# A hybrid decoder layer on one core: the low parts of the down weights by an accumulating DMA instead of a VectorE subtraction

## The chip, the cores and the metric

The kernel runs on one core of a Trainium2 chip. The core has TensorE (matmuls, into PSUM), VectorE, ScalarE and GpSimd (elementwise work), SyncE (SP, which here only issues DMAs), and 16 DMA engines that move data between HBM and the on-chip SBUF. Each engine works through its own queue of instructions in order and waits on semaphores for what other engines and DMAs produce. In the profile the engines are called PE (PEld for its weight loads), DVE, ACT, POOL and SP. The metric is the time on the device, in microseconds (us), as the median of runs; a profile is one execution of the same program, recorded instruction by instruction.

## The reference

One layer of a decoder over 256 tokens of width 1024, in float32:

```python
xn = rms_norm(x, attn_norm_g)
proj = xn @ w_in                        # one projection for both head groups
x = x + concat([y_moba, y_gla]) @ w_out # block attention and gated linear attention
hn = rms_norm(x, ffn_norm_g)
h = causal_dwconv(hn @ w_ffn_up, conv_w, conv_b)     # 2 * 2816 columns, 3 taps
x = x + (silu(h[..., :2816]) * h[..., 2816:]) @ w_ffn_down   # 2816 -> 1024
return rms_norm(x, final_norm_g)
```

The change lies in the last product, with `w_ffn_down` (2816 x 1024).

## The kernel before

**Matmuls in three parts.** TensorE takes operands of type float32r, which keep fewer bits than float32. To come close to float32, each operand is split into a high part (a copy rounded to float32r) and a low part (the operand minus its high part, again as float32r). A product is then three matmuls (`mm3`, lines 113 to 116): high by high (L114), high by low (L115) and low by high (L116), summed in PSUM. In a row such as `L115 PE MATMUL acc<-dlo,gh`, `gh` is the stationary operand and `dlo` the moving one.

**Stages.** The input projection, the two attentions and the output projection take the first 110 us or so; the FFN then runs to about 300 us. There the 2816 columns are cut into NP = 22 tiles of 128. For tile i:

- `ups[i]`, the 1 MB of up weights (128 x 2048), comes by DMA from SP into one of four `raw` buffers; ScalarE writes `hi` (L97) and VectorE `lo` (L100), in halves. The end of an up tile's second `lo` lets SP load the next up tile (`load_next`).
- `up_mm(i, ...)` multiplies them with the normed activations (`hh`, `hl`) into a PSUM bank `att`, 48 matmuls.
- VectorE rescales the result (`conv_u`, L845, or L848 in halves), ScalarE and VectorE do the convolution (`conv_a` L855, `conv_b` L863, silu L866), `gate_hi` multiplies the halves (L870) and writes the rounded gate `gh` on ScalarE (L873), `gate_lo` the rest `gl` on VectorE (L878).
- `dload(i)` has SP load the 512 KB of down weights (128 x 1024) into one of three `draw` buffers (L794). `dhi(i)` lets ScalarE write the high part into one of four `dhi` buffers (L800), `dlo(i)` lets VectorE subtract and write the low part into one of four `dlo` buffers (L805).
- `down_mm(i, tt, n)` multiplies gate and down weights for token half tt and bank n; five calls of three matmuls per tile, summed over all tiles in PSUM banks `dacc` that already hold the residual.

**Order.** In the FFN every queue's order is written out by hand; nothing is reordered. Tile 0 to 3 are unrolled (lines 938 to 1006), the rest is the loop at line 1008. In pass i TensorE does `up_mm(i)` and then `down_mm(i - 3)`; pass 4 does the down product of tiles 0 and 1 both. The other engines, in the same pass, finish tile i - 1: its conv and gate, `dhi(i - 1)` between the convolution and the gate, `dlo(i - 1)` at the end. Near the end, pass 20 also holds `dload(21)`, `dhi(20)` and `dlo(20)`, pass 21 has `dhi(21)`, and `dlo(21)` follows `conv_b(21, 1)`. After the last pass come the down products of the last four tiles, then the final norm and the stores.

**Buffers.** `dload(i)` overwrites the buffer of raw tile i - 3, so SP holds it, and everything behind it in SP's queue, until the reads of that tile by `dhi(i - 3)` and `dlo(i - 3)` are done. GpSimd has no work in the FFN.

The first tiles' order, as written (lines 980 to 1006, calls on the changed path and around it):

```python
    dhi(0); ids(1); gate_hi(0); dlo(0); gate_lo(0)               # pass 2
    ...
    hi(5, 0); conv_bb(1); conv_u(2, None); ids(2); lo(5, 0); hi(5, 1); gate_hi(1); dhi(1)   # pass 3
    conv_bb(2); gate_lo(1); gate_hi(2); dhi(2); lo(5, 1); gate_lo(2); dlo(1); dlo(2)
```

Of the kernel before, what the change touches and what calls it, by code (L numbers as in the profile page):

```python
# [12 lines left out]
AF = mybir.ActivationFunctionType  # L13
ALU = mybir.AluOpType
# [20 lines left out]
def trunk_kernel(ctx: ExitStack, tc: tile.TileContext, xT_d, wG_d, w5_d, wo_d, up_d, dn_d,  # L35
                 par_d, gla_g_d, fin_g_d, wgu_d, cos_d, sin_d, causal_d, lvl_d, ident_d, out_d):
    nc = tc.nc
    V, A, T, DMA = nc.vector, nc.scalar, nc.tensor, nc.sync
# [751 lines left out]
    downs = {}  # L790
# [6 lines left out]
    def dhi(i):  # L797
        hi = ff.tile([128, D], F32R, name="dhi", bufs=4)
        lo = ff.tile([128, D], F32R, name="dlo", bufs=4)
        A.activation(hi, downs[i][0], AF.Copy)  # L800
        downs[i] += [hi, lo]

    def dlo(i):
        d, hi, lo = downs[i]
        V.tensor_sub(lo, d, hi)  # L805

    finb = ff.tile([128, D], F32, name="finb")
    rb = ff.tile([128, S], F32, name="rb")
# [169 lines left out]
    lo(4, 1)  # L978
    conv_bb(0)
    dhi(0)  # L980
    ids(1)
    gate_hi(0)
    dlo(0)
    gate_lo(0)

# [10 lines left out]
    hi(5, 1)  # L996
    gate_hi(1)
    dhi(1)
    conv_bb(2)
    gate_lo(1)  # L1000
    gate_hi(2)
    dhi(2)
    lo(5, 1)
    gate_lo(2)
    dlo(1)
    dlo(2)

    for i in range(4, NP):
# [57 lines left out]
    for tt in range(2):  # L1066
# [4 lines left out]
        for n in range(BANKS[tt]):  # L1071
            d = dacc[tt, n]
# [91 lines left out]
```

## Time and profile before

| | before |
|---|---|
| median of 2 runs | 308.04 us (308.02 to 308.06) |
| profiled execution: span | 306.0 us |
| outside the span, against the median | 2.04 us |
| PE busy in the span | 298.6 us (98%) |
| DVE, ACT, POOL busy | 244.6, 207.3, 4.4 us |
| moved by DMA | 55.33 MB |
| low parts of the down weights (L805, DVE) | 22 x 1219 ns = 26.7 us |
| high parts of the down weights (L800, ACT) | 22 x 1047 ns = 23.0 us |

The span runs from the first to the last instruction of the profiled execution, and no time for that execution other than its span is recorded. Busy time of the engines overlaps, so the columns don't add up. In a row of a group of instructions stand line, engine, operation, output and inputs by the program's names, count, then busy time, mean duration in ns, and the idle time of the engine just before, with what ended it. In a timeline row stand start and duration in us, then engine, line, operation and names; a bracket at its end gives the idle time before it and what ended it.

### The profile page before, as it was taken

The page shows a single profiled execution, that of the slowest core. Times are in us where ns is not written, and L with a number is a line of the kernel's source. Part 1 is how long each engine was busy: PE and PEld are TensorE (multiplying, and loading weights), DVE is VectorE, ACT ScalarE, POOL GpSimd, SP SyncE. Part 2 cuts the span into 40 slices and gives each one's busy share as a digit, 9 for nine tenths or more (in the row PEclk, how much of TensorE's full clock was granted, in tenths as well). Part 3 has the DMA queues.
Part 4 walks back from the last instruction along what each step waited for, and adds up shares of the span by engine and source line. Part 5 has one row for each costly group of instructions (what it writes and reads, how often), then busy time and mean ns, then how long its engine had stood idle before and what let it go on. Part 6 is the DMA issues. An engine that isn't in the chain of part 4 may idle for free.

```text
span 306.0 us, 6251 instructions
## 1 busy us (share of the span) xinstructions
PE 298.6 (98%) x2498; PEld 282.4 (92%) x2498; DVE 244.6 (80%) x456; ACT 207.3 (68%) x385; POOL 4.4 (1%) x21
## 2 busy tenths in 40 slices
PE   8999999999999999999999999999999999999992
PEld 8999998777889999999999999999999999999992
DVE  4697998999487699799999977778888777776652
ACT  4897999898998477657677755555566665534362
POOL 2000100000000000000000000000000000000000
PEclk9999999999999999999999999999999999999999
DMA  6997855263553452981566665444444722110003
GB/s 185 372 338 283 298 177 184 97 256 141 173 203 135 179 188 72 418 349 57 200 256 256 263 216 202 161 174 167 161 178 198 274 71 69 71 69 2 0 0 138
DMA packets 12300, 55.33 MB, mean 181 GB/s; under 512 B 1376, under 2 KB 3184, under 8 KB 8048
## 3 DMA queue, kind: packets, MB, share of 16 engines
q1 hardware_dynamic: 12128, 54.81, 48.9%
q8 instruction: 19, 0.31, 0.4%
q10 hardware_dynamic: 144, 0.13, 0.1%
q14 instruction: 9, 0.07, 0.1%
HBM read 53.89 MB, written 1.05 MB: 180 GB/s over the span
## 4 chain that ended last, share of the span: by engine, by line
PE 89%; DMA 3%; ACT 3%; DVE 2%; SPq 1%; issue 1%; ACTq 0%; DVEq 0%
PE att L114 14%; PE att L116 14%; PE att L115 14%; PE acc L114 14%; PE acc L116 13%; PE acc L115 13%; DMA raw<-in_wG 3%; PE att L388 1%; DVE lo L100 1%; PE att L524 1%; ACT hi L97 1%; PE att L570 1%; PE att L452 1%; PE att L590 1%; ACT ah L181 1%
## 5 line engine op out<-in xcount | busy, mean ns | idle before, releaser
L97 ACT ACTIVATE hi<-raw 128x1024 fp32r<-128x1024 f32 (+3 forms) x88 | 79.9, 933 | 43.4 <-PE att L115 37.5
L100 DVE TENSOR_TENSOR lo<-raw,hi 128x1024 fp32r<-128x1024 f32 (+4 forms) x90 | 93.5, 1056 | 14.9 <-ACT hi L97 14.8
L114 PE MATMUL att<-hh,hi 128*128 128x256 f32 x352 | 98.5, 280 | 0.0
L115 PE MATMUL att<-hl,hi 128*128 128x256 f32 x352 | 98.2, 279 | 0.0
L116 PE MATMUL att<-hh,lo 128*128 128x256 f32 x352 | 98.2, 279 | 0.0
L114 PEld LDWEIGHTS att<-hh,hi 128*128 128x128 f32 x352 | 66.2, 188 | 0.1
L115 PEld LDWEIGHTS att<-hl,hi 128*128 128x128 f32 x352 | 66.2, 188 | 0.0
L116 PEld LDWEIGHTS att<-hh,lo 128*128 128x128 f32 x352 | 66.2, 188 | 0.0
L863 DVE SCALAR_TENSOR_TENSOR c<-us,par,c 128x256 f32<-128x256 f32 x88 | 40.7, 482 | 4.1 <-ACT c L855 2.5
L855 ACT ACTIVATE c<-us,par 128x256 f32<-128x256 f32 x44 | 24.0, 591 | 22.3 <-DVE us L845 17.0
L115 PE MATMUL acc<-dlo,gh 128*128 128x512 f32 (+1 forms) x88 | 32.2, 365 | 0.0
L116 PE MATMUL acc<-dhi,gl 128*128 128x512 f32 (+1 forms) x88 | 32.1, 365 | 0.0
L114 PE MATMUL acc<-dhi,gh 128*128 128x512 f32 (+1 forms) x88 | 32.0, 363 | 0.0
L805 DVE TENSOR_TENSOR dlo<-draw,dhi 128x1024 fp32r<-128x1024 f32 x22 | 26.7, 1219 | 0.0
L845 DVE TENSOR_TENSOR us<-att,rb 128x512 f32<-128x512 f32 x20 | 13.8, 689 | 15.3 <-PE att L116 15.3
L800 ACT ACTIVATE dhi<-draw 128x1024 fp32r<-128x1024 f32 x22 | 23.0, 1047 | 0.0
L114 PE MATMUL acc<-hi,ah 128*128 128x512 f32 x48 | 19.5, 406 | 0.0
L116 PE MATMUL acc<-hi,al 128*128 128x512 f32 x48 | 19.0, 396 | 0.0
L115 PE MATMUL acc<-lo,ah 128*128 128x512 f32 x48 | 19.0, 396 | 0.0
L115 PEld LDWEIGHTS acc<-dlo,gh 128*128 128x128 f32 x88 | 16.5, 188 | 2.0
L114 PEld LDWEIGHTS acc<-dhi,gh 128*128 128x128 f32 x88 | 16.5, 188 | 1.9
L116 PEld LDWEIGHTS acc<-dhi,gl 128*128 128x128 f32 x88 | 16.5, 188 | 1.9
(224 smaller groups left out, 505.9 us busy)
## 6 DMA issues: line engine op xcount, KB each, us to landing
raw<-in_up SPq DMA_DIRECT2D x22, 1024.0 KB, 4.8
draw<-in_dn SPq DMA_DIRECT2D x22, 512.0 KB, 5.7
raw<-in_w SPq DMA_DIRECT2D x7, 1024.0 KB, 6.0
raw<-in_wo SPq DMA_DIRECT2D x4, 1024.0 KB, 4.9
raw<-in_w SPq DMA_DIRECT2D x5, 512.0 KB, 5.3
raw<-in_wG SPq DMA_DIRECT2D x3, 528.0 KB, 8.1
raw<-in_w SPq DMA_DIRECT2D x2, 256.0 KB, 5.2
xg<-in_xT SPq DMA_DIRECT2D x1, 512.0 KB, 9.0
```

The lines of the kernel that those rows point to most:

```text
L97: A.activation(self.hi[:, a:b], self.raw[:, a:b], AF.Copy)
L100: V.tensor_sub(self.lo[:, a:b], self.raw[:, a:b], self.hi[:, a:b])
L114: T.matmul(out, sh, mh, start=first, stop=False, **kw)
L115: T.matmul(out, sh, ml, start=False, stop=False, **kw)
L116: T.matmul(out, sl, mh, start=False, stop=last, **kw)
L181: A.activation(ah[:, k], xT[:, k], AF.Copy, scale=pag[:, k:k + 1])
L388: T.matmul(p[h][64 * j:64 * j + 64, c + 32 * g:c + 32 * g + 32], k[ps, a:a + 64], q, start=True, stop=True)
L800: A.activation(hi, downs[i][0], AF.Copy)
L805: V.tensor_sub(lo, d, hi)
L845: V.tensor_tensor(u[:, :, 2:], upo[i][2].rearrange("p (a t) -> p a t", a=2), rb[:, None, :].to_broadcast([128, 2, S]), op=ALU.mult)
L855: A.activation(cv[i][:, a], u[:, a, 2:], AF.Identity, bias=par[:, P_CB + m:P_CB + m + 1], scale=par[:, P_CW + 2 * 2 * NP + m:P_CW + 2 * 2 ...
L863: V.scalar_tensor_tensor(c[:, a], u[:, a, w:w + S], par[:, wc:wc + 1], c[:, a], op0=ALU.mult, op1=ALU.add)
```

## The change

ScalarE writes, right behind the high part, a second copy with scale -1 into the buffer of the low part: the negated high part, rounded in the same way. The subtraction on VectorE is replaced by a DMA from GpSimd's queue that adds the raw down weights to that buffer, element by element, so that it again holds raw minus high part. The DMA waits for the negated copy; `down_mm` and the next user of the `draw` buffer wait for the DMA.

```diff
@@ -798,11 +798,12 @@
         hi = ff.tile([128, D], F32R, name="dhi", bufs=4)
         lo = ff.tile([128, D], F32R, name="dlo", bufs=4)
         A.activation(hi, downs[i][0], AF.Copy)
+        A.activation(lo, downs[i][0], AF.Copy, scale=-1.0)
         downs[i] += [hi, lo]
 
     def dlo(i):
         d, hi, lo = downs[i]
-        V.tensor_sub(lo, d, hi)
+        nc.gpsimd.dma_start(lo, d, accum_op=ALU.add)
 
     finb = ff.tile([128, D], F32, name="finb")
     rb = ff.tile([128, S], F32, name="rb")
```

## The prediction

> **What bounds the kernel now.** I read the page first, then the waits of TensorE, then the stages by windows, and last, instruction by instruction, the places where the down weights are split and used.
>
> ```profile
> span 306.0 us, 6251 instructions
> ...
> PE 298.6 (98%) x2498; PEld 282.4 (92%) x2498; DVE 244.6 (80%) x456; ACT 207.3 (68%) x385; POOL 4.4 (1%) x21
> ...
> PE 89%; DMA 3%; ACT 3%; DVE 2%; SPq 1%; issue 1%; ACTq 0%; DVEq 0%
> ```
>
> ```profile
> PE att L76 <- DVE warm L70: 1.0, 1, 1.0
> PE acc L717 <- ACT hi L97: 0.4, 1, 0.4
> PE att L282 <- DVE lrs L277: 0.2, 1, 0.2
> PE att L736 <- ACT hi L97: 0.2, 1, 0.2
> ```
>
> ```profile
> 250.00:280.00 30.00, 30.00 (x232) 29.19 (x232) 23.42 (x36) 15.36 (x24) 0.00 (x0) 1.00 0.15 54
> ...
> 290.00:306.00 16.00, 10.31 (x57) 9.27 (x55) 6.55 (x20) 7.84 (x19) 0.00 (x0) 0.97 0.18 66
> ```
>
> The three lines of the page say that TensorE is busy 98% of the span and holds 89% of the chain that ended last. The next four, the list of waits of TensorE, are all of them: 1.8 us, every one ahead of the FFN. In the window rows (length, then PE, PEld, DVE, ACT, POOL busy, clock, DMA share, GB/s) it fills 30.00 of 30.00 us in the FFN at clock 1.00; only after its last matmul, in the final norm and the stores, does it rest. So TensorE sets the time, and an edit to the other engines can save nothing in the FFN. It can cost: every us by which TensorE waits for an operand goes straight onto the end.
>
> The span is 306.0 us and the runs' median 308.04; 2.04 us lie outside the span. I count changes to the span and add them to 308.04. A difference under 2% (6.2 us) is taken as no change.
>
> **What is removed and added.**
>
> ```profile
> L805 DVE TENSOR_TENSOR dlo<-draw,dhi 128x1024 fp32r<-128x1024 f32 x22 | 26.7, 1219 | 0.0
> L800 ACT ACTIVATE dhi<-draw 128x1024 fp32r<-128x1024 f32 x22 | 23.0, 1047 | 0.0
> ```
>
> VectorE loses 22 subtractions of 1.22 us, 26.7 us in all. TensorE never waits for VectorE in the FFN, so by itself this is worth nothing: it moves VectorE's idle time. ScalarE gets 22 more copies of the shape in the second row, 23.0 us. In the window 250 to 280 it works 15.36 of 30.00 us, so about one more us per 8.39 us tile fits. GpSimd, nearly idle, gets 22 DMA issues. Each reads a 512 KB raw tile and the 512 KB already in dlo and writes 512 KB. What decides is when each low part is complete, since it now takes copy, GpSimd's issue and transfer one after the other. I call L the time from the end of ScalarE's negated copy to the landing of the sum, and look for the place where L has the least room.
>
> **Room at the first tiles.** Down tile 1 is read in the same pass as tile 0, so it has the shortest way.
>
> ```profile
> 132.26 1.05 ACT L800 ACTIVATE dhi<-draw 128x1024 fp32r<-128x1024 f32 x1
> 133.21 1.09 ACT L855 ACTIVATE c<-us,par 128x256 f32<-128x256 f32 x2
> 134.20 0.40 ACT L873 ACTIVATE gh<-c 128x256 fp32r<-128x256 f32 x1
> 134.63 0.42 DVE L878 TENSOR_TENSOR gl<-c,gh 128x256 fp32r<-128x256 f32 x1
> 137.53 1.10 ACT L855 ACTIVATE c<-us,par 128x256 f32<-128x256 f32 x2 [1.10 <-DVE us L845]
> 139.48 0.40 ACT L873 ACTIVATE gh<-c 128x256 fp32r<-128x256 f32 x1
> 139.78 1.05 ACT L800 ACTIVATE dhi<-draw 128x1024 fp32r<-128x1024 f32 x1
> ...
> 142.98 2.35 DVE L805 TENSOR_TENSOR dlo<-draw,dhi 128x1024 fp32r<-128x1024 f32 x2
> ...
> 143.76 0.40 PE L115 MATMUL acc<-dlo,gh 128*128 128x512 f32 x1
> 146.33 0.40 PE L114 MATMUL acc<-dhi,gh 128*128 128x512 f32 x1
> 146.56 0.39 PE L115 MATMUL acc<-dlo,gh 128*128 128x512 f32 x1
> ```
>
> A copy occupies ScalarE from 132.26 to the next start at 133.21: 0.95 us. The copy added at tile 0 therefore starts at 133.21, ends at 134.26, and pushes what is queued behind it by 0.95 us: the two conv products, then the gate's high part gh, which ended at 134.60. VectorE's gl started right on that end (134.63), so the loss passes to VectorE, and from there, through its convolution, to the ScalarE row at 137.53 that waits for VectorE's us, and on to the high part of tile 1: 139.78 becomes 140.73. The subtraction taken from VectorE at 133.34 doesn't win this back, as gl waits for gh, not for a free VectorE. Then tile 1's own copy: it starts 0.95 later, at 141.68, and ends 1.05 later, at 142.73. TensorE's first matmul on tile 1's low part stands at 146.56. The room is 146.56 - 142.73 = 3.83 us. In the kernel before, the subtraction of tile 1 (first of the two at 142.98) was done at 144.2, 2.4 us ahead. Tile 0 has 143.76 - 134.26 = 9.5 us.
>
> **The price of L.** No row shows an accumulating DMA or one from GpSimd's queue, so bounds from plain transfers.
>
> ```profile
> draw<-in_dn SPq DMA_DIRECT2D x6, 512.0 KB, 3.2
> ...
> DMA to landing us min/median/max: 3.2/5.7/10.4
> ...
> 146.00:148.00 2.00, 2.00 (x12) 1.76 (x11) 1.96 (x4) 1.97 (x3) 0.00 (x0) 1.00 0.97 389
> ```
>
> A plain 512 KB load takes 3.2 us from issue to landing in the quiet stretch from 236 us on, 5.7 in the median over the whole kernel and 10.4 at worst. At the 389 GB/s of the last row, with the DMA engines 0.97 busy, 512 KB take 1.35 us. The accumulation reads one operand more, so I add one such pass: 3.2 + 1.35 = 4.55 us alone; with the 2.5 us that sharing cost the median load (5.7 - 3.2) it is 7.05. At 142.7 sharing is partial: the load of raw tile 3 can only be issued once tile 0's sum has landed, so it is likely still moving. I take the middle, 5.8 us. What GpSimd needs to issue is in no row; the bounds 3.2 and 10.4 are meant to hold it. A gain is excluded here, since TensorE waits for nothing in this stage.
>
> The Trainium skill, page "DMA: Bandwidth & Descriptors", section "Anatomy of one DMA — SWDGE (gpsimd) path", gives a DMA from this queue as about 2.0 us plus its bytes at 436 GB/s; for 512 KB that makes 3.2 us, an estimate from the page. By it the sum would be no wait at all and 308.0 us. The row of 3.2 us agrees with it for a plain load; neither prices the accumulation.
>
> With 5.8 us tile 1's low part lands at 148.5, TensorE waits 5.8 - 3.83 = 2.0 us at 146.56, and nothing gives that back: all later matmuls are ready and follow back to back.
>
> **Room at the other places.**
>
> ```profile
> 225.60 1.05 ACT L800 ACTIVATE dhi<-draw 128x1024 fp32r<-128x1024 f32 x1
> ...
> 236.66 35.00 SPq L794 DMA_DIRECT2D draw<-in_dn  x6
> ...
> 247.28 0.40 PE L115 MATMUL acc<-dlo,gh 128*128 128x512 f32 x1
> ...
> 267.56 1.05 ACT L800 ACTIVATE dhi<-draw 128x1024 fp32r<-128x1024 f32 x1
> ...
> 283.61 1.06 ACT L800 ACTIVATE dhi<-draw 128x1024 fp32r<-128x1024 f32 x1
> 284.73 0.42 ACT L873 ACTIVATE gh<-c 128x256 fp32r<-128x256 f32 x1
> ...
> 286.75 0.42 DVE L878 TENSOR_TENSOR gl<-c,gh 128x256 fp32r<-128x256 f32 x1
> ...
> 293.90 0.39 PE L115 MATMUL acc<-dlo,gh 128*128 128x512 f32 x1
> ```
>
> Steady state, tile 13 as the example: the negated copy ends at 225.60 + 0.95 + 1.05 = 227.60. The matmuls want it at 247.28, 19.7 us later. SP's queue comes sooner: the load of raw tile 16 overwrites the buffer that the DMA reads, and starts its row at 236.66, so SP is held only if L exceeds 9.1 us. Up to then no load is late, those of the up weights queued behind it on SP included.
>
> End: for tile 21 the copy ends at 283.61 + 2.0 = 285.61, needed at 293.90: 8.29 us, with no load in flight. At 4.55 us it costs nothing. Raw tile 21 must also be there at 283.61; it can be loaded only when tile 18's sum has landed (copy ends at 267.56 + 2.0 = 269.56) and takes 3.2 us, so L may be 10.85 us. The gate of tile 20, queued behind tile 21's copy, has its high part pushed to 284.73 + 0.42 + 0.95 = 286.10, still ahead of the VectorE row at 286.75 that uses it. The last subtraction, gone from between tile 21's convolution and its rescale, frees VectorE where TensorE isn't waiting.
>
> Sum: 306.0 + 2.0 = 308.0 us of span, 308.04 + 2.0 = 310.0 us of time.
>
> **Rivals.** *No wait.* If L is at most 3.83 us, all is hidden: 308.0 us. For it: 3.2 us for a plain load. Against: the extra pass, and raw tile 3 in flight. Chance 0.20.
>
> *The accumulation is slow* (the other side). Its place is the same matmul at 146.56 and again the end; from L = 8.29 us both cost. At the worst row, 10.4 us, that is 10.4 - 3.83 = 6.6 plus 10.4 - 8.29 = 2.1 us: 316.7 us. Two percent is passed at L = 9.1 us, where 5.3 + 0.8 = 6.1. At 17 us it would be 13.2 + 8.7, thus 330 us. For it: no row shows how fast the DMA engines add, and if they read, add and write row by row, the bytes say little. Against: the end runs without other traffic, and a plain 512 KB is far below. Chance 0.20.
>
> *VectorE shuts GpSimd out.* The window row 146 to 148 has VectorE busy 1.96 of 2.00 us, so if GpSimd's descriptors had to wait for a running VectorE instruction, the 1.22 us of L805's shape (a weight split of the same size stands there) would go on top: L = 7.0, a wait of 3.2 us, 311.2 us. Against: a shared port shows nowhere, since GpSimd is idle in this stage. The Trainium skill, page "SBUF — State Buffer", section "SBUF: two separate sides", speaks against this change with such a rule: while VectorE runs an instruction in a 2-port mode, GpSimd can't write descriptors. Its condition is a one-source copy; VectorE's rows here take two tensors, and no run yet shows it. Chance 0.08.
>
> *Faster by freeing VectorE.* It would need a TensorE wait on VectorE in the FFN, and the list of waits has none: 0.02.
>
> **How the numbers follow.** The forecast (L between 3.83 and 8.29, 308.0 to 312.5 us) has 0.50, time at L = 5.8: 310.0 us. The range goes from 307.8 (no wait, with 0.2 us for the runs) to 317 (L = 10.4); what lies above 10.4 us, and faster, is left out. Slower by over 2% needs L above 9.1 us, most of the slow case: 0.18. Faster: 0.02. Within 2%: 0.80.
>
> **What would show it.** TensorE's waits after should have one line, an L115 matmul on dlo that waited for a DMA, once, about 2 us, near 146.6 us, and nothing else in the FFN; high parts of tile 1 on ScalarE near 140.7; the tile period 8.39 us before and after. The landing time of dlo's DMA is L itself: below 3.8 with no wait proves the first rival, above 8.3 with a second wait near the end the slow one. I am wrong in kind if TensorE waits in the steady state, if loads of raw tiles hold SP up, or if ScalarE doesn't reach tile 1's copy by 142.7.

## The result and the profile after

The changed kernel takes 309.97 us in the median of two runs (309.76 to 310.17), against 308.04 us before; the ratio is 1.0069 with a 95% interval of 1.0053 to 1.0085. The forecast was 310.0 us. Measured again in five executions, beside some of the variants below: 309.90 against 307.84 us, ratio 1.0062 (1.0048 to 1.0077). So the kernel is about 2 us slower, under the 2% at which a difference counts here.

The page of the changed kernel: span, busy time of the engines, and the DMA queue that is new (packets, MB, share of the 16 engines).

```profile
span 308.4 us, 6328 instructions
...
PE 298.3 (97%) x2498; PEld 282.0 (91%) x2498; DVE 221.3 (72%) x434; ACT 225.9 (73%) x407; POOL 23.0 (7%) x43
...
q0 software_dynamic: 3168, 11.54, 19.3%
```

TensorE's work is unchanged (298.3 us, 2498 matmuls). VectorE has lost 22 instructions and 23.3 us, ScalarE has gained 22 and 18.6 us of busy time, GpSimd 22 and 18.6. The 11.54 MB are the 22 sums of 512 KB.

The complete list of TensorE's waits in the changed kernel (us in all, times, longest):

```profile
PE att L736 <- ACT hi L97: 1.7, 1, 1.7
PE acc L115 <- DMA dlo<-draw: 1.5, 1, 1.5
PE att L76 <- DVE warm L70: 1.1, 1, 1.1
```

One line is new, the second: a single wait of a low-part matmul for the DMA. The first is at the start, in the input projection, long before the change; its length differs from execution to execution (0.2 us in the profile before, 0.8 in a second profile of this kernel, absent in others below). In this profile the start costs 0.6 us of the 2.4 us by which the span grew: the down product of tile 0 begins at 144.12 instead of 143.53.

The place of the wait, from the timelines of the changed kernel (start, duration, engine, line, operation):

```profile
141.32 1.05 ACT L800 ACTIVATE dhi<-draw 128x1024 fp32r<-128x1024 f32 x1
142.27 1.04 ACT L801 ACTIVATE dlo<-draw 128x1024 fp32r<-128x1024 f32 x1
...
143.62 0.86 POOL L806 DMA_DIRECT2D dlo<-draw  x1 [7.46 <-ACT c L867]
...
146.93 0.39 PE L114 MATMUL acc<-dhi,gh 128*128 128x512 f32 x1
148.77 0.50 PE L115 MATMUL acc<-dlo,gh 128*128 128x512 f32 x1 [1.46 <-DMA dlo<-draw]
149.11 0.39 PE L116 MATMUL acc<-dhi,gl 128*128 128x512 f32 x1
```

The negated copy of tile 1 ends at 143.31. TensorE's slot for the first matmul on the low part is 146.93 + 0.23 = 147.16, and it starts at 148.77: 1.61 us late. The room was 147.16 - 143.31 = 3.85 us, the latency L up to the landing about 5.4 us.

How long the sums take, by the stage in which they are issued; each line is the least, the median and the largest landing time in us, for the windows 130 to 150, 180 to 240 and 284 to 300 us of the changed kernel:

```profile
DMA to landing us min/median/max: 5.1/5.3/9.3
...
DMA to landing us min/median/max: 10.0/11.0/11.6
...
DMA to landing us min/median/max: 4.6/4.6/4.6
```

Alone, at the end, a sum lands 4.6 us after its issue; beside the loads of the loop it needs 11. From 246 us on, where the up weights are all loaded, it is 4.6 to 7.0 us.

### The profile page after: what moved, and what is told of

The parts are those of the page before. It is cut to its first block, busy times and chain, and to the rows that moved or that the text cites. A ratio compares the mean times of both kernels' runs of the same rounds, so it can differ in the third digit from the quotient of the medians.

```text
span 308.4 us, 6328 instructions
## 1 busy us (share of the span) xinstructions
PE 298.3 (97%) x2498; PEld 282.0 (91%) x2498; DVE 221.3 (72%) x434; ACT 225.9 (73%) x407; POOL 23.0 (7%) x43
## 3 DMA queue, kind: packets, MB, share of 16 engines
q0 software_dynamic: 3168, 11.54, 19.3%
## 4 chain that ended last, share of the span: by engine, by line
PE 81%; DVE 9%; ACT 4%; DMA 3%; issue 1%; SPq 1%; ACTq 0%
PE acc L114 13%; PE acc L115 12%; PE acc L116 12%; PE att L114 11%; PE att L115 11%; PE att L116 11%; DVE lo L100 4%; PE att L736 3%; DMA dlo<-draw 2%; DMA raw<-in_wG 2%; PE acc L717 1%; DVE hl L783 1%; PE att L388 1%; ACT c L856 1%; DVE xg L779 1%
## 5 line engine op out<-in xcount | busy, mean ns | idle before, releaser
L806 POOL DMA_DIRECT2D dlo<-draw x22 | 19.1, 869 | 181.9 <-ACT dlo L801 138.1
L801 ACT ACTIVATE dlo<-draw 128x1024 fp32r<-128x1024 f32 x22 | 22.9, 1042 | 0.0
```

The lines of the kernel that those rows point to most:

```text
L801: A.activation(lo, downs[i][0], AF.Copy, scale=-1.0)
L806: nc.gpsimd.dma_start(lo, d, accum_op=ALU.add)
```

## The experiments

The theory: the whole cost is one wait of TensorE, for the low part of tile 1, and all other sums are hidden. The rivals: the added DMA traffic or the use of GpSimd's queue costs by itself (at many places, at the start or at the end); or VectorE keeps GpSimd from its work. Each time is set beside one of the kernel before that was measured together with it, on the same chip.

**Tile 1 alone back on VectorE.** Against the changed kernel:

```diff
-        A.activation(lo, downs[i][0], AF.Copy, scale=-1.0)
+        if i != 1:
+            A.activation(lo, downs[i][0], AF.Copy, scale=-1.0)
...
-        nc.gpsimd.dma_start(lo, d, accum_op=ALU.add)
+        if i == 1:
+            V.tensor_sub(lo, d, hi)
+        else:
+            nc.gpsimd.dma_start(lo, d, accum_op=ALU.add)
```

> Only tile 1 goes back to VectorE's subtraction (without its negated copy); the other 21 low parts stay with the DMA. If the added time is TensorE's one wait for tile 1's sum (1.6 us of the profiled run), that wait goes: 308.0 to 308.4 us. If the cost is the 11.5 MB of added DMA traffic, or something at the start or end that comes with GpSimd's queue, 21 of 22 DMAs remain: 309.7 to 310.0 us.

308.02 us against 307.82, ratio 0.9999 (0.9987 to 1.0012). With 21 of 22 DMAs still there, no difference is left, so neither the traffic nor the queue costs more than the interval leaves open, 0.4 us. TensorE's waits hold no DMA any more.

**Tile 1's copies earlier on ScalarE.**

```diff
     conv_bb(1)
+    dhi(1)
     conv_u(2, None)
     ...
     gate_hi(1)
-    dhi(1)
     conv_bb(2)
```

> All 22 low parts by DMA, but ScalarE does the two copies of tile 1 right behind tile 1's silu, where it sat idle 1.1 us, instead of behind tile 1's gate. The negated copy should end at about 139.9 instead of 143.3 us, the sum land at about 145.5 us, ahead of TensorE: no wait, 308.0 to 308.4 us. If the cost is not this wait: 309.7 to 310.0 us.

307.71 us against 307.82, ratio 1.0000 (0.9987 to 1.0013). The timeline of this kernel's ScalarE, GpSimd and TensorE at tile 1:

```profile
137.18 1.04 ACT L800 ACTIVATE dhi<-draw 128x1024 fp32r<-128x1024 f32 x1
138.13 1.04 ACT L801 ACTIVATE dlo<-draw 128x1024 fp32r<-128x1024 f32 x1
...
139.49 0.86 POOL L806 DMA_DIRECT2D dlo<-draw  x1 [4.01 <-ACT dlo L801]
...
146.25 0.40 PE L114 MATMUL acc<-dhi,gh 128*128 128x512 f32 x1
146.48 0.39 PE L115 MATMUL acc<-dlo,gh 128*128 128x512 f32 x1
```

The sum is issued at 139.49 and lands 6.0 us later, at 145.5; TensorE takes it at 146.48 without a gap. All 22 low parts come by DMA, VectorE's busy time is 23.2 us less than before (221.4 against 244.6 us), and the time is that of the kernel before: removing the wait gives back the whole loss, and the relief of VectorE is worth nothing.

**Tile 1 alone by DMA**, all others as before (the first diff with the two cases exchanged).

> Only tile 1 uses the negated copy and the DMA. Tile 0's negated copy no longer pushes ScalarE by 0.95 us, so the copy of tile 1 should end at about 141.8 us, the sum land some 0.3 + 4.6 to 5.1 us later, and TensorE wait 0.1 to 0.6 us at 146.56: 308.2 to 308.7 us. If the room at tile 1 were not made smaller by tile 0's copy, the wait would stay 1.6 us: 309.6 us. If the cost came from all 22 DMAs together: 308.0 us and no wait.

309.32 us against 307.82, ratio 1.0047 (1.0030 to 1.0064). The wait is there with a single DMA in the kernel, but it is larger than I expected. The rows of this kernel:

```profile
142.10 0.99 POOL L810 DMA_DIRECT2D dlo<-draw  x1 [54.58 <-ACT c L871]
...
146.36 0.39 PE L114 MATMUL acc<-dhi,gh 128*128 128x512 f32 x1
147.54 0.50 PE L115 MATMUL acc<-dlo,gh 128*128 128x512 f32 x1 [0.79 <-DMA dlo<-draw]
```

The copy ended at 141.79, about 0.95 us earlier, as reckoned, but the sum took 5.4 us to land instead of 5.1, and TensorE started 0.95 us late. Being GpSimd's first DMA it also issues in 0.99 us instead of 0.86. The time grew by 1.5 us, though, not by 0.95.

To see where tile 1's room goes and whether that 0.5 us is real, four kernels were measured together: the changed one again; tile 0 wholly back on VectorE; tile 0 on VectorE, but with its negated copy left in ScalarE's queue; and tile 1 alone by DMA, again.

Both variants of tile 0 have this edit; where tile 0 is wholly on VectorE, the negated copy stands under `if i != 0:` as well.

```diff
+        if i == 0:
+            V.tensor_sub(lo, d, hi)
+        else:
             nc.gpsimd.dma_start(lo, d, accum_op=ALU.add)
```

> The changed kernel as it is, beside the variants below on one chip. TensorE waits 1.6 us at tile 1 and nowhere else in the FFN; against the kernel before +1.6 us.

> Tile 0 goes back to VectorE's subtraction without its negated copy; tiles 1 to 21 stay with the DMA. If tile 0's negated copy takes 0.95 us of tile 1's room, the wait at tile 1 falls from 1.6 to 0.65 us, plus some 0.15 us because GpSimd's first DMA issues slower (1.00 against 0.86 us): +0.7 to +1.0 us against the kernel before. If the room is not set by that copy, it stays +1.6 us.

> Tile 0 keeps its negated copy on ScalarE (VectorE's subtraction then overwrites it), but has no DMA. If the 0.95 us come from the copy in ScalarE's queue, the wait at tile 1 is back at 1.6 to 1.8 us: +1.6 to +1.8 us. If they come from tile 0's DMA and the raw load that is held behind it, the wait is as with tile 0 wholly on VectorE: +0.7 to +1.0 us.

> Only tile 1 by the DMA, again, beside the others: the profiled wait was 0.95 us, the time +1.5 us. If the wait is the whole cost, this is the same as with tile 0 alone on VectorE: +0.7 to +1.0 us; if it comes out at +1.5 us again, a part of its cost is not the wait.

| | median, us | against before (307.84) | ratio, 95% interval | TensorE's wait listed, landing at tile 1 |
|---|---|---|---|---|
| the changed kernel | 309.90 | +2.1 | 1.0048 to 1.0077 | 1.5, 5.1 us |
| tile 0 on VectorE | 309.11 | +1.3 | 1.0029 to 1.0062 | 1.5, 6.1 us |
| the same, copy kept | 309.72 | +1.9 | 1.0057 to 1.0112 | 1.8, 5.4 us |
| only tile 1 by DMA | 309.54 | +1.7 | 1.0040 to 1.0067 | 0.9, 5.5 us |

The changed kernel cost more than the 1.6 us expected; in its profile TensorE starts 1.66 us late (148.23 instead of 146.57) and the span is 1.9 us longer. With tile 0's copy in ScalarE's queue the cost is back at 1.9 us even without tile 0's DMA, as expected if the copy takes the room (two of the five executions took 311.1 and 311.5 us, and no profile shows why); without it the median falls to 1.3 us, not to the 0.7 to 1.0 us expected. In the profile of the kernel without it tile 1's copy ended at 141.86 with TensorE's row at 146.42, in the changed kernel at 142.74 with 146.34, so it had 0.96 us more room, but its sum took 6.1 us to land and used the gain up. That execution, 309.68 us, was one of the two longest of five; the other three took 308.97 to 309.11 us. Landing at the same place varied from 5.1 to 6.1 us over these profiles, and the intervals overlap, so the push by tile 0's copy is shown in the timelines but only weakly in the times.

The landings have a pattern. In the five profiles where tile 0's DMA goes ahead (the changed kernel twice, and three variants below), tile 1's sum lands in 5.1 us; in the four where tile 1's is the first DMA that GpSimd issues, it takes 5.4, 5.4, 5.5 and 6.1 us. So taking tile 0's DMA away costs a part of the room that it should give. The longer first issue, 1.00 against 0.86 us, is 0.14 us of this; what the rest is wasn't tested.

Tile 1 alone costs 1.5 and 1.7 us in the median, with TensorE 0.95 and 1.02 us late in the profiles. The profiles place most of the difference. The first profiled execution was the shortest of its four (308.89 us, the others 309.27 to 309.39); its span grew by 1.1 us, nearly all of it the wait. In the second the span grew by 1.7 us: tile 0's down product begins at 144.01 instead of 143.53 us, so 0.5 us lies ahead of it at the start, and 1.0 us in the wait. Over the profiles of this text that beginning lies anywhere from 143.21 to 144.31 us. So no profile shows a cost of this DMA beside the wait; what the other executions spent isn't recorded.

**The DMA without the addition.**

```diff
-        nc.gpsimd.dma_start(lo, d, accum_op=ALU.add)
+        nc.gpsimd.dma_start(lo, d)
```

> The DMA from GpSimd's queue copies the raw tile over the low part and doesn't add (so the low parts hold the raw weights, and the addition is left out). If the accumulation's second read is what makes the sum late, issue to landing falls from 4.6 to about 3.3 us in the quiet end, the wait at tile 1 to 0 to 0.2 us, and the landing in the steady state from 11 to about 8 us: 308.0 to 308.4 us. If GpSimd's own issue is the price, the quiet landing stays at 4.3 us or more and the wait above 1 us: 309.3 to 309.9 us.

308.01 us against 307.82, ratio 1.0009 (1.0000 to 1.0019). The group of the DMA in this kernel over the whole span, and its landing at tile 1:

```profile
L806 POOL DMA_DIRECT2D dlo<-draw x22: 527/527/662, 134.3 to 285.9; - x22
...
DMA to landing us min/median/max: 2.9/7.6/10.1
...
DMA to landing us min/median/max: 3.6/3.6/3.6
```

Alone a plain copy lands in 2.9 us, a sum in 4.6. So the addition costs 1.7 us, of which GpSimd's longer issue (0.86 against 0.53) can be 0.33 us, and the path by GpSimd's queue is no slower than the 3.2 us of SP's loads (which come from HBM, not from SBUF). In the loop, from 180 to 240 us, a plain copy lands in 8.1 us in the median, as expected, and a sum in 11.0. At tile 1 the 3.6 us fit the room, and TensorE's slot is missed by 0.07 us.

**The last sum twice.**

```diff
         nc.gpsimd.dma_start(lo, d, accum_op=ALU.add)
+        if i == NP - 1:
+            nc.gpsimd.dma_start(lo, d, accum_op=ALU.add)
```

> Tile 21's DMA is issued twice, the second one after the first has landed (its low part then holds the raw weights once too often). This doubles the last latency alone: issued at 288.2, landed at about 292.8, again issued at 293.1, landed at 297.7 us, where TensorE wants it at 296.2. If the end has the 8.3 us of room that the prediction gives, TensorE waits 1.5 us and the time is 311.3 to 311.7 us. If the end hides it anyway: 310.0 us.

311.21 us against 307.93, ratio 1.0113 (1.0096 to 1.0130), 0.1 us under the expected stretch. GpSimd's queue and TensorE near the end of this kernel:

```profile
287.47 0.86 POOL L806 DMA_DIRECT2D dlo<-draw  x1 [5.38 <-ACT dlo L801]
292.29 0.86 POOL L808 DMA_DIRECT2D dlo<-draw  x1 [3.97 <-DMA dlo<-draw]
...
295.20 0.39 PE L114 MATMUL acc<-dhi,gh 128*128 128x512 f32 x1
296.86 0.50 PE L115 MATMUL acc<-dlo,gh 128*128 128x512 f32 x1 [1.27 <-DMA dlo<-draw]
```

Doubling the latency at the end makes a second wait of 296.86 - 295.43 = 1.4 us. The room at the end is real and about as large as reckoned; a sum that lands in 4.6 us leaves some 3.4 us of it.

**Every sum from tile 3 on twice** (the same lines with `if i >= 3`).

> The DMA is issued twice, one after the other, for every tile from 3 on (their low parts then hold the raw weights once too often). GpSimd's queue then needs twice issue plus landing per tile, at least 2 x 4.9 = 9.8 us and with the loads beside it about 2 x 10 us, against a tile of 8.39 us. If the steady state has room only because each sum lands within one or two tiles, the room is eaten up and TensorE waits in most tiles: 325 to 400 us. If the DMA engines have plenty to spare and only the first tile is tight: 310 to 313 us.

347.85 us in one run. TensorE's list of waits, and three stages by windows (length, PE, PEld, DVE, ACT, POOL busy, clock, DMA share, GB/s):

```profile
PE acc L115 <- DMA dlo<-draw: 28.1, 14, 4.6
```

```profile
190.00:200.00 10.00, 9.56 (x73) 9.03 (x73) 6.16 (x10) 5.75 (x9) 2.49 (x4) 1.00 1.02 297
...
250.00:270.00 20.00, 19.35 (x128) 18.37 (x128) 8.11 (x13) 9.70 (x14) 3.49 (x4) 0.88 0.97 257
...
310.00:330.00 20.00, 9.59 (x32) 6.73 (x31) 5.16 (x12) 5.93 (x9) 4.35 (x5) 0.74 0.76 156
```

The loop's room is finite: with two sums per tile TensorE waits 14 times. The 28.1 us of waits do not make up the 40 us by which the span grew (346.0 against 306.0); in the later stages the clock granted to TensorE falls to 0.88 and 0.74, and its busy time for the same matmuls grows from 298.6 to 310.8 us. The two together, 28.1 and 12.2 us, make up the growth.

**One-source copies on VectorE beside GpSimd's issue.**

```diff
         if nxt:
             lo(i + 2, 1)
         ...
+        if i < NP - 1:
+            for _ in range(3):
+                V.tensor_copy(finb, finb)
         gate_lo(i - 1)
```

> Three one-source float32 copies of 128 x 1024 (a tile onto itself) on VectorE per tile, placed where GpSimd issues its DMA. By the rule of the Trainium skill (page SBUF - State Buffer, section SBUF: two separate sides) GpSimd can't write descriptors while such a copy runs: GpSimd's issue row would grow from 0.86 to 1.5 us or more and the landing by as much. If VectorE doesn't hold GpSimd up, the row stays 0.86 us. Either way tiles of the loop have room, so the time stays at 309.7 to 310.3 us.

309.48 us against 307.93, ratio 1.0055 (1.0040 to 1.0070): 0.2 us under the expected stretch, with the one wait at tile 1 that the changed kernel has. VectorE and GpSimd in one tile of this kernel:

```profile
229.25 2.15 DVE L1037 COPY finb<-finb 128x1024 f32<-128x1024 f32 x3
231.31 0.42 DVE L879 TENSOR_TENSOR gl<-c,gh 128x256 fp32r<-128x256 f32 x1
...
229.41 1.35 POOL L806 DMA_DIRECT2D dlo<-draw  x1 [7.05 <-ACT gh L874]
```

The issue grows from 0.86 to 1.35 us, 0.5 us, while the three copies ran for 2.15 us. One copy takes 0.69 us: the first of the three ran until 229.94, 0.53 us after GpSimd's issue had begun. So the issue grew by about what was left of the copy that was running, not by the two behind it. One issue of this kernel, at 279.01 us, began 0.13 us before the end of a copy, and it took 0.98 us, 0.12 more than 0.86. This agrees with the rule of the Trainium skill's page "SBUF — State Buffer", section "SBUF: two separate sides", which speaks of the VectorE instruction that runs; the expectation had drawn more from it. In the changed kernel itself no such copy runs in the loop, and GpSimd's issues stay at 0.86 us, at tile 1 as well as at the end.

## Why the prediction was right

**TensorE is the bound; nothing is to be gained.** Right. VectorE's 23.3 us less shortened nothing; the kernel with the copies of tile 1 moved earlier has all of the relief and none of the wait, and stands at ratio 1.0000.

**The push of 0.95 us by tile 0's copy.** Right in the timeline. Tile 1's high part was to start at 140.73; taking off the 0.59 us of the start, it started at 141.32 - 0.59 = 140.73. The room of 3.83 us measured 3.85.

**L at tile 1.** Forecast 5.8, measured 5.4 us; the wait 2.0 against 1.6 us. That the forecast of 310.0 us was met to within 0.1 us is partly luck: the wait explains 1.6 us, and in the profiled execution 0.6 us of the growth lies at the start, which the change doesn't touch. The place, the one wait and most of its size were reckoned.

**The price of an accumulating DMA.** Alone 4.55 us were forecast for L; 4.6 us from issue to landing and some 0.3 us between the copy's end and the issue were measured, thus 4.9. The addition adds 1.7 us to a plain copy, not 1.35. The estimate of 3.2 us for a DMA from this queue, from the Trainium skill's page "DMA: Bandwidth & Descriptors", section "Anatomy of one DMA — SWDGE (gpsimd) path", fits the plain copy (2.9 us alone) and not the sum.

**The steady state.** Here the step failed: I held L to be under 9.1 us in the loop, with 7.05 us at full sharing, and so no load late. From issue to landing alone it is 9.1 to 11.6 us from 152 to 240 us, and L is 0.3 us more. By the prediction's own signs, loads of raw tiles that hold SP up, it is wrong in kind here, though at no cost. The windows of the same stage, before and after:

```profile
196.00:205.00 9.00, 9.00 (x71) 8.73 (x70) 6.71 (x10) 4.79 (x7) 0.00 (x0) 1.00 0.54 190
```

```profile
196.00:205.00 9.00, 9.00 (x71) 8.73 (x70) 6.22 (x10) 6.23 (x10) 0.86 (x1) 1.00 1.01 269
```

The share of the DMA engines goes from 0.54 to 1.01, and loads and sums stretch each other: from 180 to 240 us a load of up weights lands in 10.4 us in the median, against 4.8 before. The rows of SP's waits, before and after, and of ScalarE's after show what comes of it:

```profile
SPq L794 <- DVE dlo L805: 36.6, 7, 8.0
```

```profile
SPq L794 <- DMA dlo<-draw: 74.0, 19, 8.5
...
ACT dhi L800 <- DMA draw<-in_dn: 1.6, 3, 0.8
```

SP held the load of raw down tiles 19 times, up to 8.5 us. Seven of these waits have their like in the kernel before: two at the start (among them the load of raw tile 3, which the prediction did expect to be held) and five behind 241 us, where nothing else stands in SP's queue. The other 12, from 150 to 241 us, are new: 28.9 us in all, up to 3.9 us each, and the kernel before has none there. These the prediction excluded. ScalarE waited for three of the loads, 1.6 us in all. It costs nothing, because TensorE reads the later tiles long after (19.7 us of room at tile 13, as the prediction had it), and nothing else that it reads came late. The term for sharing was sized too small, taken from a kernel whose DMA engines were half idle.

One place the prediction didn't price is tile 2. Its sum was issued at 146.72 and landed 9.3 us later, at 156.0; TensorE reads it first at 157.26, so 1.2 us were left, and this after TensorE itself had been held up by 1.6 us at tile 1. In the kernel with tile 1's copies moved earlier, where TensorE isn't held up, the same sum lands at 154.0 (145.01 + 9.0) for a matmul at 154.87: 0.9 us. At tile 3 of the changed kernel 3.6 us were left, and more at the tiles behind it. So the second place to become late is tile 2, ahead of the end, where 3.4 us were left.

**The end.** Room 8.29 us forecast; the copy of tile 21 ended at 287.94 and TensorE wanted the sum at 296.21, thus 8.27. It landed at 292.84, and TensorE didn't wait. The doubled sum confirms the limit.

**The rivals.** *No wait* would have been right for a plain copy, and the kernel without the addition shows it at 308.0 us. *The slow accumulation* was nearer than I gave it: with 11 us in the loop, the same L, 11.3 us, at tile 1 would have cost 11.3 - 3.85 = 7.5 us. It was 5.4 us there. Tile 1's sum was issued at 143.62, 1.65 us ahead of the next up load (145.27 on SP), which may be the reason, but was not tested; that lead is the same 1.65 us in the profiles where the sum took 5.4 to 6.1 us, so it doesn't explain the spread. *VectorE shuts GpSimd out* did not happen in the changed kernel (0.86 us per issue, 1.00 for the first); with one-source copies put beside it, it does, by 0.5 us.

## What to carry to other kernels

On a kernel bound by one engine, work moved off another engine is worth nothing by itself; look for the one place where the new path (copy, issue, transfer) is longer than the room. Here that was where the pipeline starts and a result is used soonest, and the tile behind it had only 1 us to spare. Price a transfer with the traffic that it adds: here a sum took 4.6 us alone and 11 us in the loop. When a start-up tile is the only late one, moving its work into an idle gap of its queue can bring the loss back, as it did here.

## What the runs showed of the hardware

- An accumulating DMA of 512 KB within SBUF, issued by GpSimd, lands in 4.6 us alone; the same as a plain copy in 2.9 us. GpSimd's issue takes 0.86 against 0.53 us, and the first one of a kernel 0.13 to 0.14 us more (1.00 and 0.66).
- Float32 copies on VectorE lengthen the accumulating issue on GpSimd by about what is left of the copy that is running when it begins: from 0.86 to 1.35 us with 0.53 us left, to 0.98 us with 0.13 us left.
- With every sum twice, TensorE's clock fell after long waits and not after short ones. After its waits of up to 2.80 us (the longest of them until 207.94) the following 3 us show 1.00. Ahead of the waits of 3.56 and 3.83 us it stood at 1.00, and in the 2 us behind each (from 248.7 and 316.6) at 0.50; after the first of the two it was 0.50 until 254 us and 1.00 again from 256 us on. In the changed kernel, with one wait of 1.6 us, the windows around it show 1.00. The Trainium skill, page "TensorE: Matmul & The Clock Gate", section "Part 1: The HAM clock gate (the "warmup" mystery)", says that an idle window of some 3.4 us halves the clock until TensorE has been busy for as long; where the clock fell agrees with this, as the waits of 2.80 and 3.56 us lie on either side of that length.
